# An RWKV-7 mixer's small TensorE products: halves of the array in turn, chunk outputs sorted by shape, a 32-row product padded to 128

## The chip, the cores and the metric

One NeuronCore of a Trainium2 chip runs the whole program: two decoder layers over 256 tokens of width 2048. The metric is the device time of one execution in microseconds.

## The reference

Layer 0 has a projection, a mixer with two head groups (a gated convolution, and RWKV-7 with 16 heads of 64), an output projection and a SwiGLU network; layer 1 has pooling and latent attention in the mixer's place. The change touches RWKV-7 only:

```python
def step(state, inp):
    r_t, w_t, k_t, v_t, kk_t, a_t = inp
    sa = jnp.einsum('bhvk,bhk->bhv', state, -kk_t)
    state = (state * w_t[:, :, None, :]
             + sa[..., None] * (kk_t * a_t)[:, :, None, :]
             + v_t[..., None] * k_t[:, :, None, :])
    y_t = jnp.einsum('bhvk,bhk->bhv', state, r_t)
    return state, y_t
...
g = jax.nn.sigmoid(xg) @ g2            # xg has 160 columns
...
y = y + bonus.reshape(bsz, s, RWKV_DIM)
return y * g
```

## The kernel before

**The frame.** Every large product is float32 made of three matmuls in a reduced float32 type: weights arrive by DMA (`w`), ScalarE makes the high part (`wh`, line 96), VectorE (DVE) the low part (`wl`, line 97). A piece of 512 columns of a weight block is called a quarter. DVE and ScalarE run up to three quarters ahead of TensorE (`self.ahead`), with six buffers of each part. In the mixer's input projection a quarter is 12 matmuls of 256 columns, in the output projection 6 of 512.

**The lane.** The mixer's small work is written as generators (`prep_a`, `prep_b`, `recur`) in a queue called the lane. After each quarter `tick` counts down, and when the count of a `yield` is up it issues the next piece of the generator. So the small products stand between quarters on TensorE, in an order that the program fixes, apart from small shifts by a scheduler that orders each engine's instructions when the program is built.

**The steps that matter here.** The sequence is cut into 4 chunks of 64 tokens; the heads are taken in two groups of 8, 2 heads to a tile of 128 partitions, one head on partitions 0 to 63 and one on 64 to 127.

- `prep_b(ti)`, for each of 8 tiles: the inner products `G` of two heads, 4 products each (64 rows of contraction, 128 columns, one per chunk). The heads are done one after the other, with a `yield` of one quarter between. DVE masks the result (`G<-sm`), ScalarE copies blocks of it to `DG`.
- `recur(grp)`, for each group, first the solve: `DG` goes to DRAM (`dN`) and comes back in another layout (`Nb`); DVE inverts 32x32 triangles in 31 steps of two instructions (`ou`, `Tb`); the result goes through DRAM again.
- Then two merges of the 32x32 inverses to 64x64 ones: 16 products of 32x32x32 per partition half, first all of one half (`b` = 0), then all of the other, into one PSUM tile (`p1`, then `p2`), each half followed by its copy on ScalarE.
- Then for each chunk: `px`, `Xs`, `pu` (eight products each, both heads of a tile in turn), the state's update `pst` (not in the last chunk) and the output `py`. For each of the 8 heads `py` issues the product with the state `st` (64 rows, from the second chunk on) and then adds the product with `UV` and `G` (128 rows).
- At the end of a group, per tile, the gate: `g2` has 160 rows; the product with rows 0 to 127 comes first, and then the one with the remaining 32, which lie on partitions 96 to 127 of `sg1` and `g2`.

All these products go through `mm` and are float32, for which the profile has two records each. PSUM tiles of the small products rotate in four buffers with the tag `sm`.

Of the kernel before, what the change touches and what calls it, by code (L numbers as in the profile page):

```python
# [18 lines left out]
P = 128  # L19
# [32 lines left out]
class Trunk:  # L52
    def __init__(self, tc, a):
        self.tc, self.nc, self.a = tc, tc.nc, a

    def mm(self, out, lhsT, rhs, start, stop):
        return self.nc.tensor.matmul(out, lhsT, rhs, start=start, stop=stop)  # L57

    def pk(self, name, j=0, n=1):
        o = PK[name][0] + j  # L60
# [406 lines left out]
    def even_mix(self):  # L467
        nc, a, tp = self.nc, self.a, self.tp
# [36 lines left out]
        def rows():  # L505
# [16 lines left out]
            out=hb, in0=self.pk("w0", 0, 16), scalar1=0.5, scalar2=None, op0=ALU.mult  # L522
# [3 lines left out]
            out=omu, in0=self.pk("mu", 0, 27), scalar1=-1.0, scalar2=1.0,  # L526
# [8 lines left out]
        st = tp.tile([P, 4, 64], F32, name="st")  # L535
        lor = tp.tile([P, T], F32, name="lor")
        sg0 = tp.tile([P, T], F32, name="sg0")
        sg1 = tp.tile([P, T], F32, name="sg1")
# [88 lines left out]
        first = {}  # L627
# [62 lines left out]
        def prep_b(ti):  # L690

            grp, i = ti // 4, ti % 4
            g = open_group(grp) if i == 0 else groups[grp]
            G, TT, UV, BKt, bv = (g[n] for n in ("G", "TT", "UV", "BKt", "bv"))
# [4 lines left out]
            for w in range(4):  # L699
# [12 lines left out]
                out=kk, in0=k, scalar=self.pk("k_k", ti), in1=pkn[:, :T],  # L712
# [3 lines left out]
            BK = BKs[i % 2]  # L716
# [28 lines left out]
                )  # L745
            S.activation(BKt[:, i], pb.rearrange("p (c n) -> p c n", c=4), AF.Copy)

            for hh in range(2):
                bs, ks = slice(hh * 64, hh * 64 + 64), slice(64 - hh * 64, 128 - hh * 64)
                hd = 2 * i + hh  # L750
                pg = self.ps()
                for c in range(4):
                    self.mm(
                        pg[:, c * P : c * P + P], BK[bs, c].rearrange("p a t -> p (a t)"),
                        ZR[bs, c].rearrange("p a t -> p (a t)"), True, True,
                    )
                V.tensor_tensor(
                    out=G[:, hd], in0=pg.rearrange("p (c n) -> p c n", c=4),
                    in1=gmask.unsqueeze(1).to_broadcast([P, 4, P]), op=ALU.mult,
                )  # L760

                for q in range(2):
                    r_ = slice(hh * 64 + q * 32, hh * 64 + q * 32 + 32)
                    S.activation(
                        g["DG"][r_, 4 * i : 4 * i + 4], G[r_, hd, :, q * 32 : q * 32 + 32],
                        AF.Copy,
                    )
                S.activation(TT[bs, i], G[bs, hd, :, 0:64], AF.Copy)
                S.activation(G[bs, hd, :, 0:64], ZR[bs, :, 0], AF.Copy)
                yield GAPS['p3']  # L770
# [4 lines left out]
        def recur(grp):  # L775
# [50 lines left out]
            for b in (0, 64):  # L826
                r1, r2 = half(b)
                V.transpose(out=Tt[r1], in_=TD[r1])
                S.activation(Tv[r1, :, 0:32], TD[r1], AF.Copy)
                S.activation(Tv[r2, :, 32:64], TD[r2], AF.Copy)  # L830
            yield GAPS['mrg0']
            for b in (0, 64):
                r1, r2 = half(b)
                for q in range(16):
                    gs = slice(q * 32, q * 32 + 32)
                    self.mm(p1[r2, gs], Tv[r1, q, 32:64], Tt[r1, q], True, True)
                S.activation(W1[r2], p1[r2].rearrange("p (g t) -> p g t", g=16), AF.Copy)
            yield GAPS['mrg']
            for b in (0, 64):
                r1, r2 = half(b)  # L840
                for q in range(16):
                    gs = slice(q * 32, q * 32 + 32)
                    self.mm(p2[r1, gs], W1[r2, q], TD[r2, q], True, True)
                S.activation(
                    Tv[r1, :, 32:64], p2[r1].rearrange("p (g t) -> p g t", g=16), AF.Copy
                )
# [3 lines left out]
            for c in range(4):  # L850
# [17 lines left out]
                if c < 3:  # L868
                    pst = self.ps()
                    for hd in range(8):  # L870
                        i, b = hd // 2, (hd % 2) * 64
                        self.mm(
                            pst[b : b + 64, i * 64 : i * 64 + 64], BKt[:, i, c, b : b + 64],
                            UV[:, hd % 2, c, i], True, True,
                        )
                py = self.ps()
                for hd in range(8):
                    i, b = hd // 2, (hd % 2) * 64
                    o = py[b : b + 64, i * 64 : i * 64 + 64]
                    if c:  # L880
                        self.mm(o, st[b : b + 64, i], ZRs[i][b : b + 64, c, 1], True, False)
                    self.mm(o, UV[:, hd % 2, c, i], G[:, hd, c, 64:128], c == 0, True)
                if c < 3:
                    src = hv(pst)
                    if c:
# [46 lines left out]
            for i in range(4):  # L932
                cs = slice(i * P, i * P + P)
                if i % 2 == 0:
                    pgt = self.ps()
                js = slice((i % 2) * T, (i % 2) * T + T)
                self.mm(pgt[:, js], g2[:, 0, cs], sg0, True, False)
                self.mm(pgt[:, js], g2[96:128, 1, cs], sg1[96:128], False, True)
                V.tensor_tensor(out=y[:, i], in0=pgt[:, js], in1=ycs[i], op=ALU.mult)


# [377 lines left out]
def layout(i):  # L1319
# [55 lines left out]
    w2a2 = np.concatenate([f["ev_w2"][0], f["ev_a2"][0]])  # L1375
    g2 = f["ev_g2"][0]
    a["lora"] = w2a2
    a["g2"] = np.stack([g2[0:128], g2[32:160]], 1).reshape(P, 2, 2, 512).transpose(2, 0, 1, 3)
    a["e_out"] = _tok(f["ev_w_out"][0])
    a["f_gate"] = np.stack([_tok(w) for w in f["ffn_w_gate"]])  # L1380
    a["f_up"] = np.stack([_tok(w) for w in f["ffn_w_up"]])
# [53 lines left out]
```

## Time and profile before

| | |
|---|---|
| median of 3 runs | 2269.24 us (2264.16 to 2272.15) |
| the profiled execution | 2269.03 us |
| its span, first to last instruction | 2267.3 us |
| mean granted TensorE clock | 0.997 of full |
| TensorE busy | 2250.6 us, 99% of the span |
| DVE / ScalarE busy | 1371.0 us, 60% / 1166.4 us, 51% |

The span is that of the profiled execution; what it lacks to that execution's time lies before the first and after the last instruction. Matmuls are pipelined, so that a record's duration is longer than the time until the next may start. Times "at" a place are microseconds from the span's start. The even mixer ends at about 520 us.

### The profile page before, as it was taken

How to read it: one execution, taken by the hardware profiler on the slowest of the kernel's cores; microseconds unless marked ns; L12 is line 12 of the kernel's file. 1: busy time of each engine (PE TensorE's matmuls, PEld its weight loads, DVE VectorE, ACT ScalarE, POOL GpSimd, SP SyncE). 2: the span in 40 equal slices, each digit the busy share in tenths (PEclk: the TensorE clock that was granted, in tenths of full speed). 3: DMA queues.
4: the chain of work that ended last, by engine and by line, in shares of the span. 5: the costliest groups of instructions: out<-in, count | busy, mean ns of one | idle time of the engine just before them, and what ended most of it. 6: DMA issues, size and time to landing. Idle time of an engine off the chain costs nothing.

```text
span 2267.3 us, 33957 instructions
## 1 busy us (share of the span) xinstructions
PE 2250.6 (99%) x12422; PEld 1921.0 (85%) x12422; DVE 1371.0 (60%) x2432; ACT 1166.4 (51%) x2085; POOL 27.1 (1%) x41
## 2 busy tenths in 40 slices
PE   9999999999999999999999999999999999999998
PEld 9999898778888888888888998788888888888886
DVE  6785477648555555555556677665555555555554
ACT  7655364546545444454555544455545444454554
POOL 0000000000000000000000000000000000000000
PEclk9999999999999999999999999999999999999999
DMA  8455235625555555555555554356555555555554
GB/s 300 134 177 166 85 132 171 196 88 185 189 191 190 192 188 194 194 187 193 188 189 190 178 171 136 117 178 208 186 194 187 189 193 193 195 187 192 188 190 154
DMA packets 124680, 405.46 MB, mean 179 GB/s; under 512 B 24896, under 2 KB 25152, under 8 KB 124128
## 3 DMA queue, kind: packets, MB, share of 16 engines
q1 hardware_dynamic: 122896, 398.31, 52.5%
q0 software_dynamic: 896, 3.80, 0.6%
q8 instruction: 97, 1.59, 0.3%
q10 hardware_dynamic: 720, 1.18, 0.1%
q14 instruction: 71, 0.58, 0.1%
HBM read 400.10 MB, written 3.15 MB: 178 GB/s over the span
## 4 chain that ended last, share of the span: by engine, by line
PE 96%; DMA 2%; DVE 1%; ACT 1%; issue 0%; SPq 0%; POOL 0%; POOLq 0%; DVEq 0%; ACTq 0%
PE mm L57 87%; PE sm L57 6%; PE sm L436 1%; DVE wl L97 1%; DMA xt<-x 0%; PE sm L198 0%; DMA Nb<-dN 0%; DMA xr<-xT 0%; DMA dN<-DG 0%; DMA pkt<-pk 0%; PE sm L1241 0%; ACT wh L96 0%; PE sm L700 0%; ACT xh L154 0%; PE sm L743 0%
## 5 line engine op out<-in xcount | busy, mean ns | idle before, releaser
L97 DVE TENSOR_TENSOR wl<-w,wh 128x512 fp32r<-128x512 f32 x1482 | 1017.3, 691 | 764.6 <-ACT wh L96 750.6
L96 ACT ACTIVATE wh<-w 128x512 fp32r<-128x512 f32 x1482 | 931.4, 631 | 952.1 <-DVE wl L97 630.1
L57 PE MATMUL mm<-wh,xh 128*128 128x512 f32 x1664 | 654.4, 393 | 2.2 <-ACT xh L151 2.2
L57 PE MATMUL mm<-wh,xl 128*128 128x512 f32 x1664 | 649.4, 390 | 1.2 <-DVE xl L152 1.2
L57 PE MATMUL mm<-wl,xh 128*128 128x512 f32 x1664 | 513.7, 390 | 0.0
L57 PEld LDWEIGHTS mm<-wh,xh 128*128 128x128 f32 x1664 | 312.9, 188 | 68.5 <-ACT xh L151 2.7
L57 PEld LDWEIGHTS mm<-wh,xl 128*128 128x128 f32 x1664 | 313.2, 188 | 64.8 <-DVE xl L152 1.5
L57 PEld LDWEIGHTS mm<-wl,xh 128*128 128x128 f32 x1664 | 312.6, 188 | 65.3
L57 PE MATMUL mm<-xh,wh 128*128 128x256 f32 x992 | 288.5, 291 | 1.3 <-ACT wh L96 1.3
L57 PE MATMUL mm<-xh,wl 128*128 128x256 f32 x992 | 282.4, 285 | 1.3 <-DVE wl L97 1.3
L57 PE MATMUL mm<-xl,wh 128*128 128x256 f32 x992 | 282.1, 284 | 0.0
L57 PE MATMUL mm<-wh,hh 128*128 128x512 f32 x704 | 274.5, 390 | 0.0
L57 PE MATMUL mm<-wh,hl 128*128 128x512 f32 x704 | 273.9, 389 | 0.0
L57 PE MATMUL mm<-wl,hh 128*128 128x512 f32 x704 | 219.9, 389 | 0.0
L57 PEld LDWEIGHTS mm<-xh,wh 128*128 128x128 f32 x992 | 190.1, 192 | 5.1 <-ACT wh L96 2.0
L57 PEld LDWEIGHTS mm<-xh,wl 128*128 128x128 f32 x992 | 189.9, 191 | 1.8 <-DVE wl L97 1.7
L57 PEld LDWEIGHTS mm<-xl,wh 128*128 128x128 f32 x992 | 190.2, 192 | 0.5
L57 PEld LDWEIGHTS mm<-wl,hh 128*128 128x128 f32 x704 | 132.2, 188 | 27.4
L57 PEld LDWEIGHTS mm<-wh,hh 128*128 128x128 f32 x704 | 132.2, 188 | 27.3
L57 PEld LDWEIGHTS mm<-wh,hl 128*128 128x128 f32 x704 | 132.2, 188 | 27.0
L228 DVE TENSOR_TENSOR h<-mm,h 128x512 f32<-128x512 f32 x54 | 34.9, 684 | 4.4 <-PE mm L57 4.3
L57 PE MATMUL mm<-lh,wh 128*128 128x256 f32 x120 | 35.4, 295 | 0.0
(256 smaller groups left out, 1279.1 us busy)
## 6 DMA issues: line engine op xcount, KB each, us to landing
w<-f_gate SPq DMA_DIRECT2D x176, 512.0 KB, 3.7
w<-f_up SPq DMA_DIRECT2D x176, 512.0 KB, 3.6
w<-f_down SPq DMA_DIRECT2D x176, 512.0 KB, 3.6
w<-e_in SPq DMA_DIRECT2D x94, 512.0 KB, 3.8
w<-e_out SPq DMA_DIRECT2D x32, 512.0 KB, 3.8
w<-o_out SPq DMA_DIRECT2D x32, 512.0 KB, 3.6
w<-o_in SPq DMA_DIRECT2D x26, 512.0 KB, 3.6
w<-e_in SPq DMA_DIRECT2D x16, 256.0 KB, 6.0
```

What stands on the lines that cost most here:

```text
L57: return self.nc.tensor.matmul(out, lhsT, rhs, start=start, stop=stop)
L96: nc.scalar.activation(hi, w[:, sl], AF.Copy)
L97: nc.vector.tensor_tensor(out=lo, in0=w[:, sl], in1=hi.bitcast(F32), op=ALU.subtract)
L228: nc.vector.tensor_tensor(out=hs, in0=ps[t], in1=hs, op=ALU.add)
L436: nc.tensor.transpose(pt[:, i * T + t * P : i * T + t * P + P], ac[t][:, (j + i) * P : (j + i + 1) * P], self.ident,)
```

## The change

The two heads' inner products of a tile are issued in turn, chunk by chunk, into two PSUM tiles; their evictions keep their places. The merges alternate between the partition halves product by product, and both copies by ScalarE follow. In `py` all state products come first and then all value products; the first product in the PSUM tile's half clears it, and the others are issued without that flag, with the check of accumulation groups switched off. The gate's second product has all 128 rows, with rows of zeros in the array that is loaded; its size is unchanged.

```diff
@@ -53,8 +53,11 @@
     def __init__(self, tc, a):
         self.tc, self.nc, self.a = tc, tc.nc, a
 
-    def mm(self, out, lhsT, rhs, start, stop):
-        return self.nc.tensor.matmul(out, lhsT, rhs, start=start, stop=stop)
+    def mm(self, out, lhsT, rhs, start, stop, shared=False):
+
+        return self.nc.tensor.matmul(
+            out, lhsT, rhs, start=start, stop=stop, skip_group_check=shared
+        )
 
     def pk(self, name, j=0, n=1):
         o = PK[name][0] + j
@@ -745,17 +748,19 @@
                 )
             S.activation(BKt[:, i], pb.rearrange("p (c n) -> p c n", c=4), AF.Copy)
 
-            for hh in range(2):
-                bs, ks = slice(hh * 64, hh * 64 + 64), slice(64 - hh * 64, 128 - hh * 64)
-                hd = 2 * i + hh
-                pg = self.ps()
-                for c in range(4):
+            pgs = [self.ps(), self.ps()]
+            for c in range(4):
+                for hh in range(2):
+                    bs = slice(hh * 64, hh * 64 + 64)
                     self.mm(
-                        pg[:, c * P : c * P + P], BK[bs, c].rearrange("p a t -> p (a t)"),
+                        pgs[hh][:, c * P : c * P + P], BK[bs, c].rearrange("p a t -> p (a t)"),
                         ZR[bs, c].rearrange("p a t -> p (a t)"), True, True,
                     )
+            for hh in range(2):
+                bs = slice(hh * 64, hh * 64 + 64)
+                hd = 2 * i + hh
                 V.tensor_tensor(
-                    out=G[:, hd], in0=pg.rearrange("p (c n) -> p c n", c=4),
+                    out=G[:, hd], in0=pgs[hh].rearrange("p (c n) -> p c n", c=4),
                     in1=gmask.unsqueeze(1).to_broadcast([P, 4, P]), op=ALU.mult,
                 )
 
@@ -829,18 +834,22 @@
                 S.activation(Tv[r1, :, 0:32], TD[r1], AF.Copy)
                 S.activation(Tv[r2, :, 32:64], TD[r2], AF.Copy)
             yield GAPS['mrg0']
+            for q in range(16):
+                for b in (0, 64):
+                    r1, r2 = half(b)
+                    gs = slice(q * 32, q * 32 + 32)
+                    self.mm(p1[r2, gs], Tv[r1, q, 32:64], Tt[r1, q], True, True)
             for b in (0, 64):
                 r1, r2 = half(b)
-                for q in range(16):
-                    gs = slice(q * 32, q * 32 + 32)
-                    self.mm(p1[r2, gs], Tv[r1, q, 32:64], Tt[r1, q], True, True)
                 S.activation(W1[r2], p1[r2].rearrange("p (g t) -> p g t", g=16), AF.Copy)
             yield GAPS['mrg']
+            for q in range(16):
+                for b in (0, 64):
+                    r1, r2 = half(b)
+                    gs = slice(q * 32, q * 32 + 32)
+                    self.mm(p2[r1, gs], W1[r2, q], TD[r2, q], True, True)
             for b in (0, 64):
                 r1, r2 = half(b)
-                for q in range(16):
-                    gs = slice(q * 32, q * 32 + 32)
-                    self.mm(p2[r1, gs], W1[r2, q], TD[r2, q], True, True)
                 S.activation(
                     Tv[r1, :, 32:64], p2[r1].rearrange("p (g t) -> p g t", g=16), AF.Copy
                 )
@@ -873,13 +882,18 @@
                             pst[b : b + 64, i * 64 : i * 64 + 64], BKt[:, i, c, b : b + 64],
                             UV[:, hd % 2, c, i], True, True,
                         )
+
                 py = self.ps()
-                for hd in range(8):
-                    i, b = hd // 2, (hd % 2) * 64
-                    o = py[b : b + 64, i * 64 : i * 64 + 64]
-                    if c:
-                        self.mm(o, st[b : b + 64, i], ZRs[i][b : b + 64, c, 1], True, False)
-                    self.mm(o, UV[:, hd % 2, c, i], G[:, hd, c, 64:128], c == 0, True)
+                for part in range(0 if c else 1, 2):
+                    for hd in range(8):
+                        i, b = hd // 2, (hd % 2) * 64
+                        o = py[b : b + 64, i * 64 : i * 64 + 64]
+                        first = i == 0 and part == (0 if c else 1)
+                        if part == 0:
+                            l, r_ = st[b : b + 64, i], ZRs[i][b : b + 64, c, 1]
+                        else:
+                            l, r_ = UV[:, hd % 2, c, i], G[:, hd, c, 64:128]
+                        self.mm(o, l, r_, first, part == 1, shared=True)
                 if c < 3:
                     src = hv(pst)
                     if c:
@@ -935,7 +949,7 @@
                     pgt = self.ps()
                 js = slice((i % 2) * T, (i % 2) * T + T)
                 self.mm(pgt[:, js], g2[:, 0, cs], sg0, True, False)
-                self.mm(pgt[:, js], g2[96:128, 1, cs], sg1[96:128], False, True)
+                self.mm(pgt[:, js], g2[:, 1, cs], sg1, False, True)
                 V.tensor_tensor(out=y[:, i], in0=pgt[:, js], in1=ycs[i], op=ALU.mult)
 
 
@@ -1375,7 +1389,8 @@
     w2a2 = np.concatenate([f["ev_w2"][0], f["ev_a2"][0]])
     g2 = f["ev_g2"][0]
     a["lora"] = w2a2
-    a["g2"] = np.stack([g2[0:128], g2[32:160]], 1).reshape(P, 2, 2, 512).transpose(2, 0, 1, 3)
+    g2r = np.concatenate([np.zeros((96, 1024), np.float32), g2[128:160]])
+    a["g2"] = np.stack([g2[0:128], g2r], 1).reshape(P, 2, 2, 512).transpose(2, 0, 1, 3)
     a["e_out"] = _tok(f["ev_w_out"][0])
     a["f_gate"] = np.stack([_tok(w) for w in f["ffn_w_gate"]])
     a["f_up"] = np.stack([_tok(w) for w in f["ffn_w_up"]])
```

On TensorE, in `recur` at the second chunk of the first group: `st` is the state, `BKt`, `ZR`, `G`, `UV` are the operands, `mm<-` stands for projection matmuls. Before:

```order
L57 MATMUL mm<-xh,wl 128x256
L57 MATMUL sm<-UV,BKt 64x64 x8
L57 MATMUL sm<-ZR,st 64x64
L57 MATMUL sm<-G,UV 64x64
L57 MATMUL sm<-ZR,st 64x64
L57 MATMUL sm<-G,UV 64x64
```

and now:

```order
L58 MATMUL mm<-xh,wl 128x256
L58 MATMUL sm<-UV,BKt 64x64 x8
L58 MATMUL sm<-ZR,st 64x64 x8
L58 MATMUL sm<-G,UV 64x64 x8
L58 MATMUL mm<-xh,wh 128x256
```

The eight pairs of a state and a value product (two of them are shown) became eight state products and then eight value products. In the same way four and four `ZR,h` products of a tile, with 12 projection matmuls between them, became eight in a row, and 16 and 16 products of a merge became 32.

On DVE, between the second group's last inner products and the first steps of its solve (`ou`, `Tb`); `wl` are low parts of projection weights, `h`, `mix` belong to the convolution. Before:

```order
L757 TENSOR_TENSOR G<-sm,cst 128x512
L608 TENSOR_TENSOR h<-h,rb_114 128x256
L757 TENSOR_TENSOR G<-sm,cst 128x512
L97 TENSOR_TENSOR wl<-w,wh 128x512
L773 TENSOR_TENSOR bv<-sm,vp_127 128x256
L97 TENSOR_TENSOR wl<-w,wh 128x512
L609 TENSOR_TENSOR mix_140<-mm,h 128x256
L97 TENSOR_TENSOR wl<-w,wh 128x512 x4
L600 TENSOR_TENSOR h<-mm,rb_115 128x256
L97 TENSOR_TENSOR wl<-w,wh 128x512 x2
L804 TENSOR_TENSOR ou<-Tb,Nb 128x31
```

and now:

```order
L611 TENSOR_TENSOR h<-h,rb_114 128x256
L762 TENSOR_TENSOR G<-sm,cst 128x512 x2
L100 TENSOR_TENSOR wl<-w,wh 128x512
L778 TENSOR_TENSOR bv<-sm,vp_127 128x256
L100 TENSOR_TENSOR wl<-w,wh 128x512
L612 TENSOR_TENSOR mix_140<-mm,h 128x256
L100 TENSOR_TENSOR wl<-w,wh 128x512 x4
L809 TENSOR_TENSOR ou<-Tb,Nb 128x31
L603 TENSOR_TENSOR h<-mm,rb_115 128x256
```

The first step of the solve moved ahead of two `wl`: before it, 191 of the program's `wl` had been issued, now 189. In the first group's solve the counts are 81 and 80. On SyncE's queue the second solve's load of `Nb` moved ahead of one load of `w`.

## Rows read from the trace of the kernel before

**Rows 1.** The page, its span and its first part: busy us, share, instructions.

```profile
span 2267.3 us, 33957 instructions
PE 2250.6 (99%) x12422; PEld 1921.0 (85%) x12422; DVE 1371.0 (60%) x2432; ACT 1166.4 (51%) x2085; POOL 27.1 (1%) x41
```

**Rows 2.** Groups by shape, TensorE: rows*columns, moving operand, xrecords; busy us, mean ns; idle.

```profile
L57 PE MATMUL sm<-ZR,h 64*128 64x128 f32 x128 | 18.5, 285 | 0.0
```

**Rows 3.** The chain from 300 to 330 us: start, us, engine, line, records.

```profile
309.86 5.76 PE mm L57 x48
...
316.05 1.08 PE sm L57 x8
317.13 1.63 PE mm L57 x12
```

**Rows 4.** TensorE in order of time, a chunk output: start, us to the last end.

```profile
226.53 0.32 PE L57 MATMUL sm<-ZR,st 64*64 64x64 f32 x2
226.78 0.33 PE L57 MATMUL sm<-G,UV 128*64 128x64 f32 x2
```

**Rows 5.** The chain from 198 to 285 us, the first group's recurrence.

```profile
202.72 1.12 PE sm L57 x32
203.84 1.02 PE mm L57 x7
...
215.93 0.61 PE sm L57 x16
...
230.70 2.52 PE mm L57 x12
233.22 1.05 PE sm L57 x16
...
242.97 1.62 PE mm L57 x12
244.60 0.62 PE sm L57 x16
...
249.08 4.11 PE sm L57 x32
...
278.94 5.91 PE mm L57 x36
```

**Rows 6.** TensorE in order of time at 47.8 us, matmuls and weight loads (PEld).

```profile
47.89 0.70 PE L57 MATMUL sm<-lor,h 64*128 64x256 f32 x4
48.53 0.27 PE L57 MATMUL sm<-cst,sq 128*128 128x2 f32 x1
...
47.89 0.30 PEld L57 LDWEIGHTS sm<-lor,h 64*128 64x128 f32 x4
```

**Rows 7.** TensorE at 272 us, the first gate (a row's first record gives the shape).

```profile
272.17 2.48 PE L57 MATMUL sm<-sg,g2w 128*128 128x256 f32 x8
274.58 0.70 PE L57 MATMUL sm<-lor,h 64*128 64x256 f32 x2
275.20 2.58 PE L57 MATMUL sm<-sg,g2w 128*128 128x256 f32 x8
```

**Rows 8.** The chain from 428 to 484 us: products of 128 rows by 256.

```profile
480.01 0.86 PE sm L57 x4
```

**Rows 9.** Stretches: engines' busy us (records), PEclk, DMA share, GB/s.

```profile
231.00:234.00 3.00, 3.00 (x28) 2.78 (x26) 0.94 (x3) 1.16 (x3) 0.00 (x0) 0.51 0.02 5
...
279.00:282.00 3.00, 3.00 (x15) 3.00 (x16) 0.65 (x3) 1.18 (x3) 1.01 (x1) 0.50 0.41 157
...
395.00:398.00 3.00, 3.00 (x7) 2.35 (x8) 3.00 (x10) 3.00 (x9) 0.00 (x0) 0.50 0.03 8
```

**Rows 10.** DVE in order of time at the second solve's start; in brackets idle, releaser.

```profile
370.21 0.19 DVE L804 TENSOR_TENSOR ou<-Tb,Nb 128x31 f32<-128x31 f32 x1 [5.61 <-DMA Nb<-dN]
```

**Rows 11.** TensorE in order of time at the same place.

```profile
371.98 0.39 PE L57 MATMUL mm<-xh,wl 128*128 128x256 f32 x1 [1.08 <-DVE wl L97]
```

## The prediction

> **What bounds the kernel now.** I read the page's first part, then the chain of work that ended last, then the order of time on TensorE in the even mixer. TensorE is busy for 99% of the span [rows 1], and the chain runs through it nearly everywhere, so a microsecond of TensorE time saved in the even mixer is a microsecond of the end unless something else becomes late there. The profiled execution took 2269.03 us for a span of 2267.3, 1.7 us outside it; the median of the runs shown is 2269.24, so the sum below is made against 2269.0.
>
> Busy time does not price the small products: neighbouring records overlap (128 records of 285 ns make 18.5 us busy [rows 2]). I price them by the chain, where a piece runs from its start to the start of the next. A float32 product leaves two records, so the 16 records of one piece are 8 products. The yardstick is a long run of projection matmuls: 48 in 5.76 us, 0.12 us each, 12 of them (one quarter of a weight block) 1.44 us [rows 3].
>
> Four things are to be seen in the small pieces.
>
> - *A change of shape is paid for.* Twelve projection matmuls right after a small piece take 1.63 us where 1.44 is their price, 0.19 us for going out and coming back [rows 3]. In the chunk output, where 64x64 state products and 128x64 value products take turns, each pair of records starts 0.25 us after the one before [rows 4], and 32 records take 4.11 us [rows 5].
> - *Sorted by shape they are cheap.* 16 records of 64x64 that alternate between the two halves take 0.61 us, and 16 of 128x64 take 0.62 [rows 5].
> - *Two products on different row halves cost what one costs.* Two products of 64 rows by 128 columns issued in turn on the two row halves (four records, at 47.89) are over after 0.64 us [rows 6]; one alone (two records, at 274.58) takes 0.62 [rows 7].
> - *Products of one half in a row don't overlap.* The eight records of an inner-product group take 1.08 us [rows 3], and 32 records on one 32x32 corner 1.12 [rows 5].
>
> **The change, part by part.**
>
> *Chunk outputs.* Six times (three chunks in each of two groups) 4.11 us become one sorted run of 16 state records (0.61) and one of 16 value records (0.62): 1.23. That saves 2.88 each, **17.3 us**. The two sorted prices are those of the same shapes and halves in the same program [rows 5], so this term is nearly sure. The first chunk has no state products and keeps its order. DVE's update of the state waits for the last product that reads the old state. That product now ends before the value products and not among the last, so this wait gets shorter, and TensorE finds its next input no later than now.
>
> *Inner products (the G matrices).* Per tile, two groups of eight records with a quarter between them (1.08 + 0.19 each, 2.54) become one group of sixteen. If the row halves overlap as the four records of [rows 6] do, it costs what one group costs, and 1.27 us go: eight tiles, **10.2 us**. If they don't overlap, sixteen records take twice 1.08 and one 0.19 is saved, 1.5 us in all. I take 10.2: [rows 6] have the same rows and columns, only a wider moving side. Their outputs lie in two PSUM buffers, as here.
>
> *Merges.* Four times, two runs of 32 records on 32x32 corners (1.12 each, and 1.02 for the 7 matmuls behind one where 0.84 is their price, so 1.30 with the change of shape [rows 5]) become one run of 64 that alternates between two corners. If the corners overlap as the 64x64 halves do, one run of 1.30 is saved each time: **5.2 us**. From the other side, the densest issue that the trace shows over a run is these 32 records in 1.12 us, 35 ns each. At that rate 64 take 2.24 us, only one change of shape is saved each time, and 0.7 us in all. I take 5.2: the 64x64 run, which alternates as the new one will, is nearest to it, and there two products cost one's columns. What waited between the two runs, a copy by ScalarE, now follows both; at least 12 matmuls stand behind them, which covers it.
>
> The Trainium skill (TensorE: Matmul & The Clock Gate, section "Wait — 56ns, not 53.3ns?") says that starts of matmuls never come closer than about 25 ns however small they are. By it, as an estimate, 64 records need 1.6 us instead of 1.1, and the four merges give 2.3 us less. The rows neither show nor exclude this, since no run of theirs comes below 35 ns in the mean.
>
> *Gate.* The 32-row product becomes one of 128 rows, of which 96 are zeros. It costs no more columns, and the loads have the same size. Eight records (four products) now take 2.41 us, from 272.17 to 274.58 [rows 7]; in one shape such a record takes 0.86 / 4 = 0.215 [rows 8], eight of them 1.72 and about 0.09 for the shape of what follows: 1.81. That saves 0.6, four times: **2.4 us**.
>
> *The clock.* The granted clock is 0.51 between 231 and 234 us, right after a chunk output, and 0.50 between 279 and 282, right after the gate [rows 9]: 1.2 GHz where the rest has 2.4. After the first, a quarter takes 2.52 us and the next run 1.05, against 1.62 and 0.62 at the same place one chunk later [rows 5]: 1.3 us. After the second, 36 matmuls take 5.91 against 4.51 (36 x 0.12 + 0.19) [rows 3, 5]: 1.4. Ahead of the first TensorE worked for 4.11 us on what takes 1.23 when sorted, ahead of the second for 2.41 twice on what should take 1.81. I expect both drops to go, **2.7 us**; the bound below is nothing, and a new drop elsewhere would cost about 1.4.
>
> *The second solve.* This is where something is lost. After the last tile's inner products a block goes to DRAM and back, and DVE stops for it at its first step of the solve: it sat idle 5.61 us before 370.21 [rows 10]. While it stands there it makes no more split weights. TensorE lives on those made ahead, and ran dry 1.08 us before 371.98 [rows 11]. In the new order two quarters fewer are split ahead of that stop. So TensorE runs dry two quarters earlier, 2 x 1.44 = 2.9 us, and what the last tile saves on it (1.27) mostly waits there too. Against that, one weight load no longer stands ahead of the returning block in the queue. The loss lies between 0.5 us (that load gave 2 us back and the solve's remaining steps run closer together) and 5 us; I take **2.5**. In the first solve DVE did not wait for the block, and the one quarter less costs nothing as long as the split weights stay ahead. Behind the second stall there is a third drop of the clock (0.50 at 395 to 398 [rows 9]), which I leave as it is.
>
> *The rest.* The evictions of the second inner product come one quarter after its matmuls. Its PSUM buffer is held that long, and of the four in rotation at most three are then taken. DVE and ScalarE do the same work in less time; where the chunk outputs stand neither is near its limit, and the work of the other layers is untouched.
>
> Sum: 17.3 + 10.2 + 5.2 + 2.4 + 2.7 - 2.5 = 35.3 us; 2269.0 - 35.3 = **2233.7 us**.
>
> **The rivals.**
>
> *Merges bound by issue.* If 64 small records can't start closer together than now, 35 ns each, 4.5 us of the 5.2 stay: 2238. For it: nothing in the trace starts faster over a run. Against it: four records on two row halves take what two on one take, also in their loads (0.30 us for four at 47.89 [rows 6]). By the page's floor, quoted above, the end would be at about 2236.
>
> *Row halves don't overlap in the inner products.* 8.7 us stay: 2242. Against it stand [rows 6].
>
> *The second solve eats more.* If the block comes back late as well, each microsecond is one of TensorE's; at 5 to 10 us more than I take, 2239 to 2244. For it: the queue is full there, and the stall is already the longest wait of this stretch that comes from memory.
>
> *Changing halves costs what changing shapes costs.* Then the kernel gets slower. In the old chunk output 15 changes cost 2.88 us, 0.19 each. The new order has 7 changes of half in each of eight inner-product groups, 31 in each of four merges and 14 in each of six chunk outputs, 264 in all. From 0.13 us a change (35.3 / 264) nothing is left, and at 0.19 the end is at about 2284. Against it: the 16 records of 0.61 us [rows 5] change halves seven times, and a price of 0.13 alone would make 0.9.
>
> **How the numbers follow.** My case has 0.64, with 2229 to 2238 of its own (the clock's two drops stay or go, the solve loses 0.5 to 5). Merges bound by issue have 0.15, the solve 0.10, row halves 0.07, changes of half 0.02, and 0.02 stay for savings that come to nothing in a way not seen here. Two executions differ by some microseconds, so the range is 2227 to 2243: it leaves out the far end of the solve's case and the last two. A measurement of this kernel tells about 0.3% (6.8 us) from no change. All cases but the last two are faster by more: faster 0.96, the same 0.02, slower 0.02.
>
> **What would show it.** In the new profile: each later chunk output as 16 records of 64x64 and 16 of 128x64 in 1.2 us; one inner-product run of 16 records in about 1.1 us per tile; one merge run of 64 records in about 1.1 us (1.6 or more would be the issue bound); gate products evenly 0.215 us apart; the clock at full speed behind chunk outputs and gate; and a wait for split weights of 3 to 5 us in the second solve. The prediction is wrong if the sorted runs keep gaps of 0.25 us, if the 16 records of an inner-product run take 2.2 us, or if the wait in the second solve is above 8 us.

## The result, and the profile after

The changed kernel takes 2228.94 us in the median of 4 runs (2228.79 to 2230.26), the kernel before 2269.85 beside it: a ratio of 0.983 by the recorded estimate (the two medians alone give 0.982), with a 95% interval of 0.9812 to 0.9847. In the sessions of the experiments the kernel before ran 50 times more, with a median of 2267.0. The profiled execution took 2228.79 us, 1.8 us more than its span.

The page, its span and its first part, answers to [rows 1]: 38.4 us of TensorE's busy time are gone, and the share is still 99%.

```profile
span 2227.0 us, 33960 instructions
PE 2212.2 (99%) x12422; PEld 1895.2 (85%) x12422; DVE 1368.3 (61%) x2432; ACT 1166.2 (52%) x2085; POOL 27.8 (1%) x41
```

The chain of work from 190 to 285 us (start, us, engine, line, records) answers to [rows 5]:

```profile
197.39 1.13 PE sm L58 x64
198.52 3.05 PE mm L58 x24
...
218.06 1.84 PE sm L58 x48
219.91 1.62 PE mm L58 x12
221.53 0.61 PE sm L58 x16
...
226.00 1.84 PE sm L58 x48
227.85 1.62 PE mm L58 x12
229.47 0.62 PE sm L58 x16
...
233.95 1.23 PE sm L58 x32
...
254.33 5.44 PE sm L58 x24
259.77 4.41 PE mm L58 x36
...
276.84 1.09 PE sm L58 x16
277.94 3.07 PE mm L58 x24
```

A merge is now one run of 64 records in 1.13 us, where 32 took 1.12. The chunk output without a state update takes 1.23 for its 32 records, where it took 4.11; with the update's 16 records ahead of it, 1.84, where before the 48 took 4.73. The quarter behind a chunk output takes 1.62 each time, where one took 2.52. The first gate, with what stands beside it, takes 5.44 where its 24 records took 6.61, and the 36 matmuls behind it 4.41 where they took 5.91. A tile's inner products are one run of 16 records in 1.09 us, where eight took 1.08 [rows 3]. Two lines of the same view of the kernel before that [rows 5] leave out:

```profile
225.98 4.73 PE sm L57 x48
...
272.33 6.61 PE sm L57 x24
```

The windows view (engines' busy us with records, PEclk, DMA share, GB/s) answers to [rows 9]: full clock behind a chunk output and behind the gate, half clock still behind the out-projection's first stalls.

```profile
219.90:222.90 3.00, 3.00 (x37) 2.80 (x36) 1.67 (x5) 1.43 (x3) 0.00 (x0) 1.00 0.56 180
259.80:262.80 3.00, 3.00 (x26) 3.00 (x26) 1.71 (x5) 1.94 (x6) 1.01 (x1) 1.00 0.44 157
368.00:371.00 3.00, 3.00 (x9) 2.32 (x8) 3.00 (x10) 2.76 (x8) 0.23 (x1) 0.50 0.04 8
```

At the second solve's start DVE in order of time (in brackets idle, releaser) answers to [rows 10]; the second fence is TensorE, where the stall of [rows 11] has no counterpart before the out-projection:

```profile
340.51 0.19 DVE L809 TENSOR_TENSOR ou<-Tb,Nb 128x31 f32<-128x31 f32 x1 [4.45 <-DMA Nb<-dN]
```

```profile
365.94 0.50 PE L58 MATMUL mm<-wh,xh 128*128 128x512 f32 x1 [1.45 <-ACT xh L154]
367.57 0.60 PE L58 MATMUL mm<-wh,xl 128*128 128x512 f32 x1 [1.13 <-DVE xl L155]
```

Where the time went is read by taking the same projection matmul in both traces (they are the same in number and order) and following how much earlier it starts. Between one piece of the lane and the next this lead stays within 0.1 us; it grows where a piece got shorter:

| stretch | expected, us | lead gained, us |
|---|---|---|
| first weights (an execution's own start) | 0 | 0.26 |
| inner products, first four tiles | 5.1 | 5.07 |
| merges, first group | 2.6 | 2.60 |
| chunk outputs, first group, with one half-clock stretch | 8.65 + 1.3 | 10.08 |
| gate, first group, with one half-clock stretch | 1.2 + 1.4 | 2.66 |
| inner products, last four tiles | 5.1 | 4.22 |
| second solve up to its merges | -2.5 | **2.42** |
| merges, second group | 2.6 | 2.66 |
| chunk outputs, second group | 8.65 | 8.68 |
| gate, second group | 1.2 | 1.66 |

The sum is 40.3, the two spans differ by 40.25. One line of what was expected has the wrong sign.

### The profile page after: what moved, and what is told of

It reads as the page before. It is cut to its first block, busy times and chain, and to the rows that moved or that the text cites. A ratio compares the mean times of both kernels' runs of the same rounds, so it can differ in the third digit from the quotient of the medians.

```text
span 2227.0 us, 33960 instructions
## 1 busy us (share of the span) xinstructions
PE 2212.2 (99%) x12422; PEld 1895.2 (85%) x12422; DVE 1368.3 (61%) x2432; ACT 1166.2 (52%) x2085; POOL 27.8 (1%) x41
## 4 chain that ended last, share of the span: by engine, by line
PE 98%; DVE 1%; DMA 1%; ACT 0%; issue 0%; POOLq 0%; POOL 0%; DVEq 0%
PE mm L58 90%; PE sm L58 5%; PE sm L439 1%; PE sm L201 0%; DVE wl L100 0%; DMA w<-e_in 0%; ACT wh L99 0%; PE sm L1255 0%; DMA pkt<-pk 0%; PE sm L746 0%; PE sm L703 0%; DVE h L607 0%; ACT o L366 0%; ACT DG L769 0%; DVE Tb L813 0%
```

## Experiments

The theory for the small products: a change of shape is paid for and a change of the half or corner is not, two products on different halves take the time of one, and the four edits add up. Its rivals are those of the prediction, and that the edits get in each other's way. For the second solve two theories stood against each other once the result was known. *The residual load:* POOL loads 1 MB of the residual (`h<-x`) as soon as the last inner products are done, because its buffer is theirs. Before, that is 1.1 us before the block goes out (351.62 and 352.75 us), and both are on the way together; now the last products are done while an eviction of theirs, and with it the block, still comes a quarter later: the load starts 5.1 us before the block (325.35 and 330.44), and of its 8.0 us to landing 2.9 are left. *The queue:* one weight load fewer stands ahead of the block's return on SyncE's queue. The two issues, before and now:

```profile
351.62 0.88 POOL L976 DMA_DIRECT2D h<-x  x1 [27.01 <-PE sm L57]
352.75 0.38 SPq L784 DMA_DIRECT2D dN<-DG  x1
```

```profile
325.35 0.88 POOL L990 DMA_DIRECT2D h<-x  x1 [19.36 <-PE sm L58]
330.44 0.38 SPq L789 DMA_DIRECT2D dN<-DG  x1
```

### Each edit alone

**e1_outputs_sorted**: the kernel before with the sorted chunk outputs and nothing else.

```diff
+                for part in range(0 if c else 1, 2):
+                    for hd in range(8):
...
+                        self.mm(o, l, r_, first, part == 1, shared=True)
```

> Only the chunk outputs are sorted by shape; all else is as before. By the sum of the prediction: each later chunk output 1.23 us instead of 4.11, 17.3 us in all, and the clock's drop behind the first of them gone (1.3 us), so 18.6 us less, about 2250.5. The second solve should stay as it was: DVE idle some 5.6 us before its first step, TensorE dry for about 1 us at its start. The rival, that what the sorted products save waits in the second solve or at the output projection, expects less than 14 us.

Measured 2246.76 us against 2267.83, ratio 0.9918 (0.9903 to 0.9933): 21.1 us. Each later chunk output takes 1.23 us, and no half-clock stretch follows one. That is 2.5 more than expected, and the solve did not stay as it was: its block is back after 15.3 us, where the recorded execution of the kernel before took 17.45, and TensorE does not run dry at its start. Nor is there a half-clock stretch behind the first gate, though the gate is the old one here.

**e2_merges_in_turn**: the merges alone.

```diff
+            for q in range(16):
+                for b in (0, 64):
...
+                    self.mm(p1[r2, gs], Tv[r1, q, 32:64], Tt[r1, q], True, True)
...
```

> Only the merges alternate between the corners. If corners overlap: four runs of 64 records of 1.13 us, 5.2 us less, about 2264. If 64 records can't start closer together than 35 ns each: runs of 2.2 us and 0.7 us less, about 2268.5.

Measured 2260.3, ratio 0.9977 (0.9963 to 0.9992): 7.5 us, more than the 5.2 of the edit. By the lead of the projection matmuls the four merges give 1.31, 1.30 and together 2.66, 5.3 in all; the rest is the clock and the solve's start, which vary (below); the ten executions lie between 2258.47 and 2271.08.

**e3_inner_in_turn**: the inner products alone.

```diff
+            pgs = [self.ps(), self.ps()]
+            for c in range(4):
+                for hh in range(2):
...
```

> Only the inner products are issued in turn; the second solve's first step and its load of the block move ahead as in the whole change. The prediction's working: 10.2 us saved and 2.5 lost in the second solve, 7.7 less, about 2261.5. The theory after the result: the block comes back sooner, since the 1 MB load of the residual, which waits for the last inner product, now starts 4 to 5 us ahead of the block's way out instead of 1 us; DVE then waits less, TensorE does not run dry at the solve's start, and some 12 to 13 us are saved, about 2257.

Measured 2258.39, ratio 0.9967 (0.9955 to 0.9979): 9.4 us. That lies between the two expected gains, 7.7 and 12 to 13. Each tile gains 1.27 by the same lead; 0.9 are lost again within the last four. The solve's block is back 9.6 us after it goes out (346.55 to 356.19), where the recorded execution of the kernel before took 17.45 (352.75 to 370.21), although nothing of the solve was edited: the residual load starts at 341.5, 5 us before the block, and TensorE does not run dry at the solve's start. This was the first sign against the prediction's step.

**e4_gate_padded**: the padded gate alone.

```diff
-                self.mm(pgt[:, js], g2[96:128, 1, cs], sg1[96:128], False, True)
+                self.mm(pgt[:, js], g2[:, 1, cs], sg1, False, True)
...
```

> Only the gate's second product has 128 rows. 0.6 us less per half group, 2.4 in all, and the clock's drop behind the first group's gate gone (1.4 us): 3.8 less, about 2265.5. The rival, that the drop stays (its cause being the many products with one wide shape and not the 32-row ones), expects 2.4 less and the drop still there, about 2267. Rows of zeros are added to the array that is loaded; the values are the same.

Measured 2267.45, ratio 0.9999 (0.9984 to 1.0014): nothing that can be told. The lead shows the gate's gain, 2.66 at the first (with the half-clock stretch behind it gone) and 1.65 at the second, and where it went: 1.44 are gained behind the first group's first later chunk output, which has full clock here, but 1.35 and 2.99 are lost at the two that follow, 1.2 at the out-projection's start and 1.5 near 460 us, all at half clock. The windows of this run (columns as above):

```profile
241.00:244.00 3.00, 3.00 (x22) 2.77 (x24) 1.32 (x4) 1.43 (x3) 0.00 (x0) 0.55 0.02 5
251.00:258.00 7.00, 7.00 (x32) 6.00 (x31) 1.02 (x2) 1.43 (x3) 0.00 (x0) 0.54 0.19 68
...
279.00:282.00 3.00, 3.00 (x23) 2.67 (x24) 1.49 (x6) 1.67 (x5) 1.01 (x1) 1.00 0.50 175
```

Up to the gate, at 272 us in the kernel before, this program has the same TensorE instructions in the same order, and yet the half-clock stretches stand at the second and third of these chunk outputs instead of the first. Which of the slow chunk outputs is followed by one is not fixed by the program.

**e10_changed_but_old_gate**: so the gate was taken out of the whole change instead.

```diff
-                self.mm(pgt[:, js], g2[:, 1, cs], sg1, False, True)
+                self.mm(pgt[:, js], g2[96:128, 1, cs], sg1[96:128], False, True)
...
```

> The changed kernel with the gate's second product back on 32 rows (partitions 96 to 127), everything else as changed. Alone in the kernel before, the padded gate gained nothing that can be told (0.4 us of 2268), since stretches at half clock appeared elsewhere. If the gate's price is real and only covered up there, undoing it here costs 2.4 us (four times 0.6), and 3.8 if a half-clock stretch behind the gate returns with it: 2231 to 2233. Rival: the padding is worth nothing in this program, 2228.5 to 2229.5, and the chain still shows six products behind one another at the same spacing.

Measured 2232.24 (2230.99 to 2233.14), 3.3 us above the changed kernel; ratio to the kernel before 0.9842 (0.9828 to 0.9855), where the changed kernel has 0.983. The two were measured at different times, and the two intervals overlap, so the time alone does not show the gate. Its chain does: the two gates are back at their old price (5.44 and 4.35 in the changed kernel). No half-clock stretch follows the first, old as it is:

```profile
253.93 6.61 PE sm L58 x24
260.53 1.54 PE mm L58 x12
...
457.34 5.71 PE sm L58 x24
```

That is 1.17 and 1.36, 2.5 us; by the lead of the projection matmuls 1.17 and 1.64, 2.8. The gate's price is real, and alone it was covered up by the clock.

### Turns, or only joining?

**e8_joined_without_turns**: the changed kernel with the two heads' inner products and the merges' halves joined, but one half after the other.

```diff
-            for c in range(4):
-                for hh in range(2):
+            for hh in range(2):
+                for c in range(4):
...
-            for q in range(16):
-                for b in (0, 64):
+            for b in (0, 64):
+                for q in range(16):
```

> The changed kernel with the joined runs but without turns: eight inner products of a tile in one run, first the four of one half, then the four of the other; the merges' 32 products in one run, first 16 of one corner, then 16 of the other. If the gain of both is overlap: inner runs of 2.0 to 2.2 us and merge runs of 2.1 to 2.2, so 8.4 and 4.3 us slower than the changed kernel, about 2241.5. If it was mostly the changes of shape saved: within 2 us of the changed kernel.

Measured 2237.31, 8.4 us above the changed kernel; ratio to before 0.9865 (0.9847 to 0.9882). Its chain:

```profile
200.26 2.04 PE sm L58 x64
202.29 3.05 PE mm L58 x24
...
281.53 1.64 PE sm L58 x16
283.17 3.07 PE mm L58 x24
```

A merge without turns takes 2.04 (1.13 in turn), an inner-product run 1.64 (1.09). Four times 0.91 and eight times 0.55 make 8.0. In turn, the second half is free: TensorE's records start in pairs, one of each half 6 to 7 ns apart, and 16 take what eight took.

The expectation of 12.7 took for granted that without turns nothing overlaps, and the trace shows that something still does. Records of one half alone start 0.11 us apart. Of the 16 here, the first line below has the four that start before 282.01 us, the second the five from 282.45 on. The other seven start in the 0.44 us between, where one half alone has four: the second half's first record starts at 282.02, 5 ns after the first half's fifth, and four records of each pass side by side.

```profile
281.46 0.71 PE L58 MATMUL sm<-ZR,h 64*128 64x128 f32 x4
...
282.45 0.72 PE L58 MATMUL sm<-ZR,h 64*128 64x128 f32 x5
```

At 0.11 us each, sixteen with no overlap would take 1.08 + 8 x 0.11, about 1.98. So the 1.27 us per tile divide into 0.9 for the overlap and 0.37 for going in and out of the shape once instead of twice. Eight records' own 0.9 are most of the 1.08 of a short run [rows 3]; the rest of it, 0.19, and the 0.19 in the quarter behind it are the change of shape.

### The second solve

**e7_after_residual_collides**: the changed kernel with the residual load held until the block is ready, so that both go out together, as before.

```diff
+            if grp == 1:
+                V.tensor_copy(out=self.h[:, 1, 0:1], in_=g["DG"][:, 15, 0:1])
             dN = self.dp.tile([16, P, 32], F32, tag="dN", name="dN")
```

> The changed kernel, with the residual's load made to wait for the last block row that the inner products leave (one column copied by DVE), so that it starts within about 1 us of the block's way out, as it did before the change. Orders as in the changed kernel. Theory: the round trip grows from 10.1 us to 15 to 17, and TensorE runs dry for 3 to 6 us at the start of the solve, as the prediction had expected: 2.5 to 6 us slower than the changed kernel. Rival (only the weight load's place in the queue matters): round trip stays at 10 to 11 us and the time within 1 us.

Measured 2232.62 (2231.79 to 2233.43), 3.7 us above the changed kernel and 4.4 above e6 (below), which was measured beside it; ratio to before 0.9848 (0.983 to 0.9867). DVE and TensorE at the solve's start:

```profile
344.52 0.19 DVE L811 TENSOR_TENSOR ou<-Tb,Nb 128x31 f32<-128x31 f32 x1 [7.63 <-DMA Nb<-dN]
```

```profile
345.80 0.38 PE L58 MATMUL mm<-xh,wl 128*128 128x256 f32 x1 [1.85 <-DVE wl L100]
```

This is the stall that the prediction forecast, of 1.85 us where it had 3 to 5: the block is late and TensorE, with two quarters fewer made ahead, runs dry.

**e5_before_late_residual** and **e6_after_late_residual**: the kernel before, and the changed one, with the load held until the block is back.

```diff
             eng = V
+            if grp == 1:
+                V.tensor_copy(out=self.h[:, 1, 0:1], in_=Nb[:, 0, 0:1])
             for m in range(31):
```

> The kernel before, with the 1 MB load of the first half of the residual made to wait until the second solve's block is back (one copy of one column by DVE, written into the residual's place ahead of the load). All orders stay as before: 191 low parts ahead of the solve's first step, two weight loads between the block's way out and its load. Theory (the residual's load delays the block): the way from the block's issue to the first step falls from 17.5 us to about 11 to 13, TensorE's 1.1 us without work at the start of the solve goes, and 2 to 4 us are saved. Rival (the second weight load ahead of the block's load delays it): 17 us or more, and no gain.

> The changed kernel with the same delay of the residual's load. Theory: the round trip of 10.1 us gets little shorter (to about 9 to 10), since in the changed kernel the load was nearly over when the block went out; time within 1 us of the changed kernel's.

Measured 2262.04 for e5, ratio 0.9982 (0.9972 to 0.9992), 4.5 us below the kernel before; in its trace the stall at the solve's start and those at the out-projection's start are gone. Its first 340 us show something else. TensorE's instructions are those of the kernel before, in the same order, and still the half-clock stretches behind the first later chunk output and behind the first gate [rows 9] are missing; the quarter there takes 1.63 us and the 36 matmuls 4.41 (2.52 and 5.91 before):

```profile
231.20:234.20 3.00, 3.00 (x35) 2.80 (x36) 1.71 (x5) 1.41 (x3) 0.00 (x0) 1.00 0.03 5
278.00:281.00 3.00, 3.00 (x26) 3.00 (x26) 1.71 (x5) 1.93 (x5) 1.01 (x1) 1.00 0.44 158
```

Measured 2228.23 for e6 (2227.27 to 2228.52), ratio to before 0.9827 (0.9812 to 0.9843), which can't be told from the changed kernel.

**e11_second_load_ahead**: e6 with the returning loads three quarters later in the program, so that the second half of the block stands behind a second weight load.

```diff
+            if grp == 1:
+                yield 3
             for p in range(2):
                 nc.sync.dma_start(
                     out=Nb[p * 64 : p * 64 + 64],
```

> The changed kernel with the late residual load, and the loads of the returning block delayed by three quarters in the program, so that one half of the block stands behind two weight loads on SyncE's queue (as both halves do in the kernel before with the late load) and the other behind one, as in the changed kernel. With the late load the kernel before had the block back 12.3 us after it was sent, the changed kernel after 9.3. Theory that the second weight load ahead makes that difference: the first step of the solve comes 11.5 to 13 us after the block is sent. Rival that the difference has another source (where the split weights stand, how full the queue was): 9 to 10.5 us. The time is within 2 us of the run with the late load in either case, since the split weights made ahead cover it.

The block is back after 12.7 us (332.31 to 344.99), as the queue's theory wants. The time is 2232.08 (2231.78 to 2232.41), 3.8 above e6, where I expected at most 2. The recorded executions differ by 4.5, and by the lead the late block costs nothing at the solve's start: 1.4 are lost in the first 25 us, which the edit does not touch, 1.8 at the out-projection's start, and 1.3 over the second group's later pieces, which the `yield` also moves against the quarters.

The issues of the block in five runs (queue, form, count, KB, median us to landing): the kernel before, the changed one, e7, e5 and e11.

```profile
Nb<-dN SPq DMA_DIRECT2D x2, 256.0 KB, 9.8
dN<-DG SPq DMA_DIRECT2D x1, 256.0 KB, 6.9
```

```profile
Nb<-dN SPq DMA_DIRECT2D x2, 256.0 KB, 4.7
dN<-DG SPq DMA_DIRECT2D x1, 256.0 KB, 4.5
```

```profile
Nb<-dN SPq DMA_DIRECT2D x2, 256.0 KB, 9.2
dN<-DG SPq DMA_DIRECT2D x1, 256.0 KB, 3.3
```

```profile
Nb<-dN SPq DMA_DIRECT2D x2, 256.0 KB, 7.6
dN<-DG SPq DMA_DIRECT2D x1, 256.0 KB, 3.4
```

```profile
Nb<-dN SPq DMA_DIRECT2D x2, 256.0 KB, 6.8
dN<-DG SPq DMA_DIRECT2D x1, 256.0 KB, 3.2
```

With the table of the whole trip (from the block's issue to the first step of the solve) they divide the matter:

| run | residual load, against the block's issue | weight loads ahead of the return | trip, us |
|---|---|---|---|
| before, recorded execution | 1.1 us earlier | 2 | 17.45 |
| e1, e2, e4, solve as before | 1.1 us earlier | 2 | 15.2 to 15.3 |
| e5, before with the load late | after the return | 2 | 12.3 |
| changed, e3, e10 | 5.1 us earlier | 1 | 9.6 to 10.1 |
| e8 | 3.9 us earlier | 1 | 11.1 |
| e7 | 0.8 us later | 1 | 13.3 |
| e6 | after the return | 1 | 9.3 |
| e11 | after the return | 1 and 2 | 12.7 |

Each line is of single executions. The kernel before's 17.45 did not repeat: e1, e2 and e4, with the same solve, take 15.2 to 15.3, with the same way out (6.8 us) and a return that is 2 us shorter; what made it longer stays open. Measured from them, a residual load that starts with the block costs 3 us of the trip (against e5; e7 against the changed kernel 3.2), and a second weight load ahead about 3 as well (against e6: e11 3.4, on one half alone; e5, which differs by the four edits too, 3.1). Both theories hold, each for its part: from 15.2 the trip loses 2.9 to e5, and 3.1 from there to e6, and the changed kernel's early residual load takes 0.8 back, which leaves 10.1.

### A version beyond the change

**e9_values_first_late_load**: the late load, and in each later chunk output the value products first, which have the update's shape.

```diff
-                for part in range(0 if c else 1, 2):
+                for part in ((1, 0) if c else (1,)):
...
```

> The changed kernel with two edits: the residual load waits until the second solve's block is back (as in the run with the late load), and in each later chunk output the value products (128 rows) come before the state products (64 rows). The state update's own products have 128 rows too and stand right ahead, so the piece has one change of shape less. Theory that each change of shape costs about 0.1 us on its own (0.19 for going out and coming back): six chunk outputs save 0.1 to 0.6 us each where the update stands ahead (four of the six, since the last chunk of a group has no update), together with the late load 0.5 to 2 us under the changed kernel, about 2227. Rival: the order of the two runs is free of charge, because going out to 64 rows and back is paid once in either order, or the state products, which now end last, hold DVE's update of the state by 0.6 us and it shows: 2228 to 2230.

Measured 2228.3 (2227.7 to 2230.15), ratio to before 0.9828 (0.9815 to 0.9841): no better than the changed kernel that can be told. Its chain shows the change of shape saved, 1.70 for the 48 records where the changed kernel takes 1.84; four such pieces are worth 0.6 us. In the second group they are not gained: by the lead against e6 0.3 is lost each time behind the next piece, whose 16 `UV,G` records are split there, two of them 1.15 us ahead of the other 14 with three projection matmuls between.

```profile
217.55 1.70 PE sm L58 x48
219.25 1.63 PE mm L58 x12
```

## Why the prediction was right, and where it was wrong

*Chunk outputs, 17.3: right.* 8.63 and 8.68 by the lead (the first with its clock taken off), 17.3. The rule behind it stands too: records that change their half every time cost nothing extra, and records that change between 64 and 128 rows do. But the 2.88 us are not all the 15 changes (0.19 each). Sorted, the records of two halves start in pairs 6 to 7 ns apart; in the alternation each starts alone. What e9 saves with one change is 0.14; by that 15 are worth 2.1, and the other 0.7 is overlap that the alternation had prevented. That a value product adds to the words that the state product has just written is not the cause: from one shape to the other the start takes 0.15 us in the alternation and also in the sorted run, where those words were written 0.5 us before. The Trainium skill (TensorEngine Tiling (Array Packing), section "Key Properties") says that changing the tiling mode drains the engine, as distinct from changing only the tile within a mode. These rows agree, in that a change costs 0.14 and a change of half none.

*Inner products, 10.2: right*, but for 0.9. 9.29 came: the last four tiles give 0.85 less than the first, and 0.8 of that goes at two places where TensorE starts a piece late: at 304.96 us it has waited for ScalarE's `vx`, at 323.28 for DVE's `h`. That these engines had more time for it when the heads stood a quarter apart is argued and not shown. The prediction looked at DVE and ScalarE where the chunk outputs stand ("neither is near its limit") and not here. Its reason, overlap, is the larger part (0.9 of 1.27 a tile, at e8); its bound without overlap, 1.5 us for all, was too low, since a joined run spares 0.37 a tile, 3.0.

*Merges, 5.2: right.* 5.26 came. 64 records in 1.13 us are 18 ns apart in the mean, so neither the rival of 35 ns nor the floor of 25 ns that the prediction quoted from the Trainium skill (TensorE: Matmul & The Clock Gate, section "Wait — 56ns, not 53.3ns?") binds for 32x32 products on alternating corners; here the measurement decides. (The prediction's estimate by that floor, 2.3 us less, should be 1.9: four times the 0.48 by which 1.6 exceeds 1.12.)

*Gate, 2.4: right*, 2.5 by e10's chain and 2.8 by its lead.

*The clock, 2.7: the amount by luck.* The recorded executions differ by 2.9 there (1.45 and 1.5), and the changed kernel's has no half-clock stretch behind the lane's pieces. But e5 has neither stretch with these pieces as they were, e1, e3 and e10 have none behind the old gate, and in e2 to e4 such stretches stand at other places, at 1.2 to 1.5 us each or twice that. So the reason, that the pieces' shape changes make the drops, is not shown for these two. A part of the gain may be real: the granted clock, averaged over an execution, is 0.996 in the median of the kernel before's 50 (0.990 to 0.998) and 0.997 to 0.999 in the changed kernel's four. Among the 50, those with 0.995 take 2269.3 us in the mean and those with 0.997 2265.5.

*The second solve, -2.5: wrong in sign; this is the failed step.* The lead grows there by 2.42. I counted two quarters fewer made ahead as TensorE's loss "2 x 1.44 = 2.9 us", and took the block's trip as it was, but for a weight load that "gave 2 us back". The split weights are indeed fewer (e7 shows that loss at once, when the trip is 3.2 us longer), but the trip is 7.4 us shorter than in the recorded execution before, 5.1 shorter than in e1, e2 and e4. What I missed is a transfer on POOL's queue: I followed the rows that the new order moves on DVE and SyncE, and not the load that the end of the last inner products *releases*. The weight load is worth 3 us of the trip and not 2.

Not all of the 2.42 is the change's. By the out-projection's start (394 us before) e1, e2 and e4, whose solve is as before, are ahead of the recorded execution by 2.2 to 2.3 over the same stretch, the changed kernel by 2.4; the stall of [rows 11], 1.35 by the lead, is missing in all of them. Then those three lose 1.0 to 1.2 in a half-clock stretch of 6.8 us, where the kernel before and the changed one have 3.4. So the change itself gains between 0.2 and 1.4 us there. With that in place of -2.5 the sum is 38.0 to 39.2, 2231.0 to 2229.8 us; the loss that was forecast did not come.

The four edits alone give 21.1, 7.5, 9.4 and 0.4, 38.4 in sum, and 40.9 together by the medians. They add up within what a measurement tells, though each alone is off by the clock's wandering, and the kernel before that each is set against has medians of 2266.5 to 2269.9 from session to session.

## What to carry to other kernels

Price a small TensorE piece by the time from its start to the next piece's start: going into another shape and back, and each change between, cost more here than the products themselves in the chunk outputs, and products on different halves or corners in turn took the time of one. Before counting a half-clock stretch as a saving, look at a second execution: here both came and went without any edit. When an edit ends a piece earlier, look for every transfer that the piece's buffers release, on each queue, and ask what round trip it will now miss or meet. When several edits each remove a little, test one by taking it out of the whole as well: alone, the gate's 2.5 us could not be seen.

## What the runs showed that was not expected

A 256 KB block's way out to DRAM took 3.2 to 3.4 us with nothing of POOL's beside it (e5, e6, e11) and 6.8 to 6.9 with the 1 MB load started 1.1 us before (the kernel before, e1, e2, e4). With that load started 0.8 us after it (e7) the way out took 3.3, and the two halves of the return 9.0 and 9.4 behind one weight load. Without POOL's load on the way, each half of the return, 256 KB too, took 4.4 to 5.4 us behind one weight load (the changed kernel, e6) and 7.3 to 8.1 behind two (e5, e11).

Half-clock stretches moved between executions of the same TensorE instructions (e4 against the kernel before up to the first gate, e5 up to the second solve), each worth 1.2 to 1.5 us of TensorE's time or twice that.

Records of two row halves that are issued in turn start 6 to 7 ns apart. Issued one half after the other they still overlap where the halves meet, by four records: sixteen of 64 rows by 128 columns take 1.64 us, where eight take 1.08 and eight more at their spacing of 0.11 would add 0.9.
